# Block products from the ninth and the fifth feature tile on, h shifted by ScalarE, and two side jobs moved into the down projections

## The chip, the cores and the metric

The kernel runs on one core of a Trainium2 chip. Five engines with queues of their own work at once: TensorE (PE in the profile; its weight loads are listed apart as PEld), VectorE (DVE), ScalarE (ACT), GpSimd (POOL) and SyncE (SP), which here issues nearly all transfers. The metric is the device time of one execution in microseconds, taken as the median of several runs.

## The reference

One layer of a streaming encoder with 512 tokens and a model width of 1024, in float32:

```
mod = silu(c) @ w_ada + b_ada                      # nine vectors of 1024: shift, scale, gate, three times
x += 0.5 * g1 * SwiGLU(rms(x) * (1 + s1) + sh1)    # first FFN,  1024 -> 2 x 2816 -> 1024
x += g2 * mixer(rms(x) * (1 + s2) + sh2)           # gated DeltaNet heads and latent attention heads
x += 0.5 * g3 * SwiGLU(rms(x) * (1 + s3) + sh3)    # second FFN, same sizes
SwiGLU(h) = (silu(h @ w_gate) * (h @ w_up)) @ w_out
```

The change touches the two FFNs and the small work that runs beside them, not the mixer itself.

## The kernel before

**Layout.** Everything is kept transposed: 128 features on the partitions, the 512 tokens along the free dimension. So h is eight tiles of 128x512, and the 2816 hidden features are 22 feature tiles, numbered from 0.

**Precision.** Each float32 operand is split into a rounded part and a rest, and each product is three matmuls: high by high, high by low, low by high (`mm3`, L447 to L449). h is held as pairs hh, hl. `modulated` makes them: VectorE scales x into a scratch tile hm (L639), ScalarE adds the shift and rounds to hh (L641), VectorE makes hl (L633). A weight tile is split by ScalarE (a rounding copy, L217) and VectorE (the rest, L218).

**Ordinary feature tiles** (`plain`, and the end of `by_sevens`): gate and up are two accumulators, each of 8 x 3 matmuls of 512 columns. `glu` applies silu on ScalarE (L808) and multiplies on VectorE (L810). There are three accumulators in PSUM for all of this.

**Product tiles** (`by_sevens`, `seven_products`, `sevenths`): gate and up together are seen as a 2 by 2 block matrix, tokens halved as well, and are made from seven block products instead of eight, each of 4 x 3 matmuls of 256 columns (L335). For this VectorE and ScalarE form four sums of weight blocks (s12, s34; L252, L256, L267, L276), and `combined` forms once per FFN four sums of blocks of h, the tiles t7. `combined` first gets h back as hh + hl (L303). `SEVEN` holds the range of feature tiles that are done so: 9 to 18 in the first FFN, 5 to 18 in the second. Tiles 0 to 2 of the first FFN are done by the opening stage (`phase0`), 19 to 21 are ordinary again; during those `parted` splits all finished activations (`glu_parts`, L816, L817).

**Down projections** (`down`): eight output tiles, each of three weight units with 8, 8 and 6 of the 22 feature tiles, three matmuls of 512 columns for each. At the end VectorE adds the gated result to x (L922); the second FFN then transposes and stores the tile (`store`, L992, L994). The last output tile is done in two halves.

**Side work.** Small jobs are written as generators and put into `Side` lists, which the loops step between groups of matmuls; `Rates` steps a list at a given rate. They are:
- `ada_rest`: the remaining columns of `mod`. It streams w_ada (tiles ar), accumulates it on VectorE (aa, L762, L764), sums over partitions with TensorE (L783), copies the row out of PSUM (rw, L786) and transposes it (L790). Group 0 holds the first gate, group 3 the last gate, which `down` of the second FFN needs.
- `mixer_consts`: positions, cosine and sine tables and gains for the mixer; 14 small loads, 58 VectorE instructions, 32 small fills on GpSimd.

Group 0 runs beside the ordinary tiles of the first FFN, groups 1 and 2 in its down projection. `mixer_consts` runs beside tiles 19 to 21 of the first FFN, group 3 beside tiles 19 to 21 of the second and the start of its down projection.

**Order.** A planner orders each engine's instructions, in the main by their place in the program, and takes later ones first where it holds earlier ones to be unready. `in_order`, `behind` and `queued` fix the order of some of them. Tiles come from pools: 56 slots of 128x512 for h, activations and scratch, four buffers each for raw, high and low weights; the pools early (first column group) and seven (weight sums) follow each other in the same memory.

Of the kernel before, what the change touches and what calls it, by code (L numbers as in the profile page):

```python
# [20 lines left out]
NT = 512  # L21
# [8 lines left out]
SEVEN = range(9, 19), range(5, 19)  # L30
# [59 lines left out]
class Block:  # L90
# [201 lines left out]
    def combined(self):  # L292

        nc, v = self.nc, self.nc.vector
        f = lambda x: x.bitcast(F32)
# [3 lines left out]
        for j in range(4):  # L299
            x = []  # L300
            for h in (self.h[j], self.h[j + 4]):
                x.append(self.slot(s="hx"))
                v.tensor_tensor(out=x[-1], in0=f(h[0]), in1=f(h[1]), op=ALU.add)  # L303
# [173 lines left out]
    def phase0(self):  # L477
# [66 lines left out]
        nc.vector.tensor_tensor(out=hl, in0=m, in1=hh.bitcast(F32), op=ALU.subtract)  # L544
        nc.vector.tensor_tensor(out=wl, in0=raw0, in1=wh.bitcast(F32), op=ALU.subtract)
        raw(*tiles[7])
        pu = [self.acc() for _ in range(3)] + [self.aux() for _ in range(3)]
        for kt in range(KT):
# [9 lines left out]
            for j in range(6):  # L558
# [4 lines left out]
                if j == 2 and more:  # L563
                    columns(kt + 1, *cols)
                    self.modulate([kt + 1], slice(0, NT), rb, self.c2, self.c1)
                    if kt == 0:
                        w = weights(kt + 1)
# [35 lines left out]
    def new_h(self):  # L603
        self.h = [(self.slot(F32R, "hh"), self.slot(F32R, "hl")) for _ in range(KT)]

# [16 lines left out]
    def modulate(self, kts, ts, rb, scale, shift):  # L622
        drain(self.modulated(kts, ts, rb, scale, shift))

    def modulated(self, kts, ts, rb, scale, shift):
# [5 lines left out]
        def low(kt, t):  # L631
            hh, hl = self.h[kt]
            nc.vector.scalar_tensor_tensor(out=hl[:, ts], in0=t[:, :w], scalar=shift[:, kt:kt + 1],  # L633
# [3 lines left out]
        for kt in kts:  # L637
            t = self.slot(s="hm")
            nc.vector.scalar_tensor_tensor(out=t[:, :w], in0=self.xT[kt][:, ts], scalar=scale[:, kt:kt + 1], in1=rb[:, :w],  # L639
                                           op0=ALU.mult, op1=ALU.mult)  # L640
            nc.scalar.activation(self.h[kt][0][:, ts], t[:, :w], AF.Identity, bias=shift[:, kt:kt + 1])  # L641
# [40 lines left out]
    def norm_half(self, half, pc, j):  # L682
# [10 lines left out]
        yield from self.modulated(range(KT), ts, rb, self.mod[j + 1], self.mod[j])  # L693
# [83 lines left out]
    def ada_columns(self, g, accs):  # L777
# [8 lines left out]
        nc.vector.tensor_copy(rw[:32 * n, :], pr[:32 * n, :])  # L786
# [48 lines left out]
    def ffn1(self):  # L835
# [1278 lines left out]
```

## Time and profile before

| | us |
|---|---|
| median of three runs | 1058.62 (1057.68 to 1059.16) |
| profiled execution, its own time | 1057.94 |
| span of its profile | 1056.2 |
| first FFN, product tiles 9 to 18 | 133.1 to 234.0 |
| first FFN, tiles 19 to 21 | 234.0 to 267.3 |
| first down projection | from 267.3 |
| second FFN, product tiles 5 to 18 | 748.8 to 889.9 |
| second FFN, tiles 19 to 21 | 889.9 to 925.8 |
| second down projection and stores | from 925.8 |

Times inside the span count from its start. In a group row the columns are line, engine, operation, tiles, count, then busy time and mean duration, then the idle time ahead of it and what ended that. In a timeline row they are start, duration, engine, line, tiles. Matmuls overlap, so the distance of their starts is what they cost, not their listed duration. In a row of windows stand the stretch, its length, then busy time (and count) of TensorE, its weight loads, VectorE, ScalarE and GpSimd, the granted TensorE clock, the busy share of the DMA engines and GB/s.

### The profile page before, as it was taken

The page shows a single profiled execution, that of the slowest core. Times are in us where ns is not written, and L with a number is a line of the kernel's source. Part 1 is how long each engine was busy: PE and PEld are TensorE (multiplying, and loading weights), DVE is VectorE, ACT ScalarE, POOL GpSimd, SP SyncE. Part 2 cuts the span into 40 slices and gives each one's busy share as a digit, 9 for nine tenths or more (in the row PEclk, how much of TensorE's full clock was granted, in tenths as well). Part 3 has the DMA queues.
Part 4 walks back from the last instruction along what each step waited for, and adds up shares of the span by engine and source line. Part 5 has one row for each costly group of instructions (what it writes and reads, how often), then busy time and mean ns, then how long its engine had stood idle before and what let it go on. Part 6 is the DMA issues. An engine that isn't in the chain of part 4 may idle for free.

```text
span 1056.2 us, 16319 instructions
## 1 busy us (share of the span) xinstructions
PE 1035.7 (98%) x6417; PEld 904.3 (86%) x6417; DVE 722.5 (68%) x1280; ACT 471.2 (45%) x857; POOL 25.2 (2%) x74
## 2 busy tenths in 40 slices
PE   6999999999999999999999989999999999999998
PEld 5788799998887798888788769998999999778887
DVE  4479978769888547558787477788688886842221
ACT  3342345555222225469864554354455556422221
POOL 0000000000100000100000001100000000000000
PEclk8999999999999999999999999999999999999999
DMA  9988234343789435211232021113333344723320
GB/s 276 285 260 278 82 100 119 102 121 91 256 287 339 130 96 158 78 40 41 61 80 66 21 80 41 40 42 99 98 103 101 102 119 141 227 76 111 112 62 30
DMA packets 208028, 130.74 MB, mean 124 GB/s; under 512 B 13890, under 2 KB 192079, under 8 KB 207951
## 3 DMA queue, kind: packets, MB, share of 16 engines
q1 hardware_dynamic: 207950, 129.69, 41.3%
q8 instruction: 50, 0.82, 0.3%
q14 instruction: 28, 0.22, 0.1%
HBM read 127.18 MB, written 2.49 MB: 123 GB/s over the span
## 4 chain that ended last, share of the span: by engine, by line
PE 89%; DVE 5%; ACT 2%; DMA 2%; issue 2%; SPq 0%; POOL 0%; DVEq 0%; POOLq 0%; ACTq 0%
PE pa L447 18%; PE pa L448 18%; PE pa L449 18%; PE pa L335 13%; PE pb L335 10%; PE pb L447 1%; PE pb L448 1%; PE pb L449 1%; PE pb L596 1%; PE pb L1847 1%; DVE wl L218 1%; PE pb L1827 1%; DMA xt<-in_x 0%; DVE cv L1391 0%; ACT bd L1477 0%
## 5 line engine op out<-in xcount | busy, mean ns | idle before, releaser
L217 ACT CAST wh<-wr 128x1024 fp32r<-128x1024 f32 (+1 forms) x116 | 116.4, 1008 | 245.8 <-PE pa L448 216.7
L218 DVE TENSOR_TENSOR wl<-wr,wh 128x1024 fp32r<-128x1024 f32 (+1 forms) x116 | 135.3, 1169 | 117.5 <-ACT wh L217 113.3
L447 PE MATMUL pa<-hh,wh 128*128 128x512 f32 (+1 forms) x453 | 174.8, 386 | 1.6 <-ACT sg L808 1.6
L448 PE MATMUL pa<-hl,wh 128*128 128x512 f32 (+1 forms) x453 | 172.8, 381 | 0.0
L449 PE MATMUL pa<-hh,wl 128*128 128x512 f32 (+1 forms) x453 | 172.7, 381 | 0.0
L447 PE MATMUL pa<-ah,wh 128*128 128x512 f32 (+1 forms) x396 | 146.6, 370 | 0.0
L449 PE MATMUL pa<-ah,wl 128*128 128x512 f32 (+1 forms) x396 | 144.9, 366 | 0.0
L448 PE MATMUL pa<-al,wh 128*128 128x512 f32 (+1 forms) x396 | 144.8, 366 | 0.0
L447 PEld LDWEIGHTS pa<-hh,wh 128*128 128x128 f32 x453 | 85.3, 188 | 20.7 <-ACT sg L808 3.0
L449 PEld LDWEIGHTS pa<-hh,wl 128*128 128x128 f32 x453 | 85.3, 188 | 15.8 <-DVE wl L218 0.4
L448 PEld LDWEIGHTS pa<-hl,wh 128*128 128x128 f32 x453 | 85.4, 188 | 14.3 <-DVE hl L633 0.2
L447 PEld LDWEIGHTS pa<-ah,wh 128*128 128x128 f32 x396 | 74.7, 189 | 14.3 <-ACT wh L217 1.7
L449 PEld LDWEIGHTS pa<-ah,wl 128*128 128x128 f32 x396 | 74.7, 189 | 12.3
L448 PEld LDWEIGHTS pa<-al,wh 128*128 128x128 f32 x396 | 74.7, 189 | 11.8
L764 DVE SCALAR_TENSOR_TENSOR aa<-ar,sc,aa 128x512 f32<-128x512 f32 x98 | 73.0, 749 | 9.3 <-DMA ar<-in_w_ada 7.7
L252 DVE TENSOR_TENSOR wl<-sf,wh 128x1024 fp32r<-128x1024 f32 x48 | 58.6, 1222 | 30.0 <-ACT wh L256 30.0
L335 PE MATMUL pa<-hh,wh 128*128 128x256 f32 x192 | 54.5, 284 | 0.0
L335 PE MATMUL pa<-th,wh 128*128 128x256 f32 x192 | 54.3, 283 | 0.0
L335 PE MATMUL pa<-tl,wh 128*128 128x256 f32 x192 | 54.3, 283 | 0.0
L335 PE MATMUL pa<-th,wl 128*128 128x256 f32 x192 | 54.3, 283 | 0.0
L335 PE MATMUL pa<-hl,wh 128*128 128x256 f32 x192 | 54.3, 283 | 0.0
L335 PE MATMUL pa<-hh,wl 128*128 128x256 f32 x192 | 54.3, 283 | 0.0
(434 smaller groups left out, 2214.1 us busy)
## 6 DMA issues: line engine op xcount, KB each, us to landing
wr<-in_ffn_w_in SPq DMA_DIRECT2D x79, 512.0 KB, 3.8
ar<-in_w_ada SPq DMA_DIRECT2D x80, 256.0 KB, 5.9
ar<-in_w_ada SPq DMA_DIRECT2D x32, 512.0 KB, 7.6
wr<-in_ffn_w_out SPq DMA_DIRECT2D x32, 512.0 KB, 3.9
wr<-in_w_in SPq DMA_DIRECT2D x21, 512.0 KB, 3.7
wr<-in_ffn_w_out SPq DMA_DIRECT2D x16, 384.0 KB, 3.6
wr<-in_w_out SPq DMA_DIRECT2D x8, 512.0 KB
wr<-in_ffn_w_in SPq DMA_DIRECT2D x8, 384.0 KB, 7.0
```

Of the source, the lines that this page charges most:

```text
L217: self.nc.scalar.copy(hi, raw)
L218: self.nc.vector.tensor_tensor(out=lo, in0=raw, in1=hi.bitcast(F32), op=ALU.subtract)
L252: sub = lambda out, x, y: nc.vector.tensor_tensor(out=out, in0=x, in1=y, op=ALU.subtract)
L335: nc.tensor.matmul(z, a[:, j, :], b, start=start and j == 0 and i == 0, stop=j == 3 and i == 2, skip_group_check=not start)
L447: mm(out, wh, xh, start=start, stop=False)
L448: mm(out, wh, xl, start=False, stop=False)
L449: mm(out, wl, xh, start=False, stop=stop)
L596: nc.tensor.matmul(pg[32 * q:32 * q + 32, :256], self.sc[:, kc:kc + 1].to_broadcast([P, 32]), a[:, kc], start=(e == 0), stop=(e == 1), til ...
L764: nc.vector.scalar_tensor_tensor(out=acc, in0=a, scalar=sc, in1=acc, op0=ALU.mult, op1=ALU.add)
L1827: nc.tensor.matmul(ps[:, :n], self.qnT[h][:, ts], self.knT[h][:, :n], start=True, stop=False)
L1847: nc.tensor.matmul(po[:, :P], pT[:, b * P:(b + 1) * P], v[b][:, h * P:(h + 1) * P], start=(b == 0), stop=(b == i))
```

## The change

- `SEVEN` begins one tile earlier in both FFNs: tile 8 in the first and tile 4 in the second become product tiles. The ordinary stretches ahead of them shorten by one tile, and the rates of the side work there are set anew; the first column group is flushed one tile earlier.
- `combined` no longer adds hh + hl on VectorE. `modulated` keeps its scratch tile hm (`self.kept`), and ScalarE adds the shift to it in place. For tile 0 of the first FFN the already shifted tile m is kept.
- In `ada_columns`, ScalarE copies the row out of PSUM in place of VectorE.
- `mixer_consts` moves from tiles 19 to 21 into output tiles 3 and later of the first down projection.
- Group 3 of `ada_rest` moves into output tiles 0 and 1 of the second down projection, at three steps a part. These two tiles' results stay in their accumulators until the gate is there; stores run one tile later.
- In the last product tile the next weight unit is split as that tile's third side step, not ahead of it, and the raw weights of the next tile are requested one tile earlier.

```diff
-SEVEN = range(9, 19), range(5, 19)
+SEVEN = range(8, 19), range(4, 19)
...
     def combined(self):
...
-            for h in (self.h[j], self.h[j + 4]):
-                x.append(self.slot(s="hx"))
-                v.tensor_tensor(out=x[-1], in0=f(h[0]), in1=f(h[1]), op=ALU.add)
+            for k in (j, j + 4):
+                t, shift = self.kept[k]
+                if shift is not None:
+                    nc.scalar.activation(t, t, AF.Identity, bias=shift)
+                x.append(t)
...
     def modulated(self, kts, ts, rb, scale, shift, keep=False):
...
-            t = self.slot(s="hm")
+            if not keep:
+                t = self.slot(s="hm")[:, :w]
+            else:
+                if ts.start == 0:
+                    self.kept[kt] = self.slot(s="hm"), shift[:, kt:kt + 1]
+                t = self.kept[kt][0][:, ts]
...
     def ada_columns(self, g, accs):
...
-        nc.vector.tensor_copy(rw[:32 * n, :], pr[:32 * n, :])
+        nc.scalar.copy(rw[:32 * n, :], pr[:32 * n, :])
...
     def ffn1(self):
...
-            self.plain(act, 3, 5, Rates((side,), (0.75,)))
-            self.plain(act, 5, 6, Rates((side, sums), (0.75, 1)))
-        self.plain(act, 6, 8, Rates((side, sums), (1, 1)))
+            self.plain(act, 3, 4, Rates((side,), (0.75,)))
+            self.plain(act, 4, 6, Rates((side, sums), (0.75, 1)))
+        self.plain(act, 6, 7, Rates((side, sums), (1, 1)))
         side.flush()
         self.late_exit()
         self.seven_enter()
-        self.plain(act, 8, 9, sums, True)
+        self.plain(act, 7, 8, sums, True)
         sums.flush()
-        consts = Side()
-        consts.add(self.mixer_consts())
-        self.by_sevens(act, SEVEN[0], consts, 12)
-        consts.flush()
+        self.by_sevens(act, SEVEN[0])
...
     def by_sevens(self, act, fs):
...
+        def first():
+            yield
+            yield
+            self.prefetch(1)
...
             else:
-                self.prefetch(1)
+                side.add(first())
+            if f + 2 == fs.stop:
+                self.preload(2)
...
     def down(self, act, gate, norm=None):
...
+        side, held = Side(), []
+        side.add(self.ada_rest((1, 2) if norm else (3,), True))
+        consts = Side()
         if norm:
-            side = Side()
-            side.add(self.ada_rest((1, 2), True))
+            consts.add(self.mixer_consts())
         for t in range(last):
             if norm and t == 1:
                 self.masks()
-            for i, _ in enumerate(parts(t, full)):
-                side.step((2, 2, 2)[i])
-                if not norm and i == 1 and t > 0:
-                    self.store(t - 1, range(NB))
+            for i, _ in enumerate(parts(t, full, late=not norm and t < 2)):
+                side.step(2 if norm else 3)
+                if t > 2:
+                    consts.step()
+                if not norm and i == 1 and t > 2:
+                    self.store(t - 2, range(NB))
+            if not norm and t == 1:
+                side.flush()
+                for h in held:
+                    finish(*h)
+                self.store(0, range(NB))
...
     def ffn2(self, norms):
...
-        self.plain(act, 2, 4, Rates((side,), (2,)))
-        self.plain(act, 4, 5, side, True)
+        self.plain(act, 2, 3, Rates((side,), (3,)))
+        self.plain(act, 3, 4, side, True)
         side.flush()
-        others = Side()
-        others.add(self.ada_rest((3,), True))
-        self.by_sevens(act, SEVEN[1], others, 8)
-        self.down(act, 8, side=others)
+        self.by_sevens(act, SEVEN[1])
+        self.down(act, 8)
```

More of the change, by code (lines that the diff above doesn't have):

```diff
@@ L692, in norm_half @@
         yield
-        yield from self.modulated(range(KT), ts, rb, self.mod[j + 1], self.mod[j])
+        yield from self.modulated(range(KT), ts, rb, self.mod[j + 1], self.mod[j], j == 6)
     def first_units(self, units, lag, norms):
@@ L913, in by_sevens, with down @@
         side.flush()
-    def down(self, act, gate, norm=None, side=None):
+    def down(self, act, gate, norm=None):
         nc = self.nc
@@ L928, in finish, with parts @@
                 self.square_in(t, ts, accum)
-        def parts(t, ts, units=None, by=8):
+        def parts(t, ts, units=None, by=8, late=False):
             p = self.acc()
@@ L936, in parts @@
                     yield
-            if norm and ts != full:
+            if late:
+                held.append((t, ts, p))
+            elif norm and ts != full:
                 update(t, ts, p)
@@ L956, in down @@
             for i, _ in enumerate(parts(last, ha, units)):
-                if i == 1:
-                    self.store(last - 1, range(NB))
+                if i < 2:
+                    self.store(last - 2 + i, range(NB))
             for i, _ in enumerate(parts(last, hb, units)):
```

22 lines of the change are left out of this document (10 added, 12 removed).

## The prediction

> **What bounds the kernel now.** I read the page first (busy shares and the chain), then TensorE's waits, then the instructions of each stage in order of time, then the stages' busy times.
>
> ```profile
> span 1056.2 us, 16319 instructions
> PE 1035.7 (98%) x6417; PEld 904.3 (86%) x6417; DVE 722.5 (68%) x1280; ACT 471.2 (45%) x857; POOL 25.2 (2%) x74
> PE 89%; DVE 5%; ACT 2%; DMA 2%; issue 2%; SPq 0%; POOL 0%; DVEq 0%; POOLq 0%; ACTq 0%
> ```
>
> TensorE is busy for 98% of the span and holds 89% of the chain that ended last. So the time falls only by TensorE work taken out or by holes closed, and it rises wherever an engine that feeds TensorE comes late. Outside the mixer there are few holes. The largest is in the view of TensorE's waits, and the timelines of TensorE and ScalarE show its place:
>
> ```profile
> PE pa L447 <- ACT sg L808: 1.6, 2, 1.4
> 906.00 0.39 PE L449 MATMUL pa<-hh,wl 128*128 128x512 f32 x1
> 907.80 0.50 PE L447 MATMUL pa<-hh,wh 128*128 128x512 f32 x1 [1.41 <-ACT sg L808]
> 907.15 0.59 ACT L808 ACTIVATE sg<-pa 128x512 f32<-128x512 f32 x1
> 247.46 0.59 ACT L808 ACTIVATE sg<-pa 128x512 f32<-128x512 f32 x1
> 918.91 1.05 PE L783 MATMUL pb<-aa,ones 128*32 128x512 f32 x2
> 920.17 0.50 PE L447 MATMUL pa<-hh,wh 128*128 128x512 f32 x1 [0.22 <-ACT sg L808]
> 936.79 0.98 PE pb L783 x2
> 889.88 0.40 PE L447 MATMUL pa<-hh,wh 128*128 128x512 f32 x1
> 925.75 0.39 PE L447 MATMUL pa<-ah,wh 128*128 128x512 f32 x1
> ```
>
> The hole lies in the second FFN, in the three ordinary feature tiles behind the block products (889.88 to 925.75). Tile 20's second projection needs the accumulator that tile 19's gate still holds, until ScalarE runs its silu (L808) at 907.15. In the first FFN the same silu runs at 247.46, and TensorE does not wait. Starts there are normally 0.23 us apart, so the hole is 907.80 - 906.00 - 0.23 = 1.57 us. At 918.91 a pair of column sums and its hole take 1.26 us to the next start, where such a pair takes 0.98 (the row at 936.79): 0.28 us more.
>
> **Block products in two more tiles.** The price of a tile is read from starts, because matmuls overlap and their mean length is no price.
>
> ```profile
> 250.98 0.39 PE L447 MATMUL pa<-hh,wh 128*128 128x512 f32 x1
> 267.08 0.39 PE L449 MATMUL pa<-hh,wl 128*128 128x512 f32 x1
> 133.10 0.28 PE L335 MATMUL pa<-hh,wh 128*128 128x256 f32 x1
> 141.90 2.88 PE pa L335 x24
> 151.98 2.88 PE pa L335 x24
> 748.79 1.43 PE pa L335 x12
> ```
>
> From 250.98 to 267.08 lie 72 matmuls without a break: 16.10 / 71 = 0.2268 us each. An ordinary tile has 2 x 8 x 3 = 48 of them, 10.88 us. A product tile has 7 x 4 x 3 = 84 matmuls of 256 columns; the same product returns after 151.98 - 141.90 = 10.08 us, 0.120 us each. So each converted tile saves 0.80 us of TensorE, and two save 1.60 us. Weight bytes stay the same. The Trainium skill, TensorE: Matmul & The Clock Gate, Back-to-back issue gap, gives N / 2.4 + 2.5 ns for one warm matmul: as an estimate 215.8 and 109.2 ns here, 10.36 against 9.17 us a tile and 2.4 us saved, which would make the total 0.8 us lower. The trace's 226.8 and 120.0 ns lie 11 ns above both, and the sum goes by the trace.
>
> What this costs is cover. The first product tile comes 10.88 us earlier, with less VectorE time ahead of it.
>
> ```profile
> 62.00:122.40 60.40, 60.40 (x270) 49.02 (x270) 53.44 (x80) 20.67 (x28) 0.00 (x0) 1.00 0.76 235
> 122.40:133.20 10.80, 10.80 (x51) 8.92 (x50) 10.80 (x21) 3.85 (x6) 0.00 (x0) 1.00 0.25 74
> 143.30:153.40 10.10, 10.10 (x87) 10.10 (x86) 8.31 (x13) 5.54 (x10) 0.00 (x0) 1.00 0.35 101
> 716.00:738.00 22.00, 22.00 (x99) 18.22 (x98) 21.66 (x40) 10.19 (x15) 0.00 (x0) 1.00 0.28 80
> 130.44 1.22 DVE L252 TENSOR_TENSOR wl<-sf,wh 128x1024 fp32r<-128x1024 f32 x1
> 744.29 1.23 DVE L252 TENSOR_TENSOR wl<-sf,wh 128x1024 fp32r<-128x1024 f32 x1 [0.95 <-ACT wh L256]
> 122.40 1.28 DVE L303 TENSOR_TENSOR hx<-hh,hl 128x512 f32<-128x512 f32 x2
> L786 DVE COPY rw<-pb x4: 681/684/691, 121.8 to 937.8; 128x512 f32<-128x512 f32 x3, 64x512 f32<-64x512 f32 x1
> L218 DVE TENSOR_TENSOR wl<-wr,wh 128x1024 fp32r<-128x1024 f32 x93 | 113.3, 1222 | 71.1 <-ACT wh L217 69.2 <-PE pb L1528 0.7
> L641 ACT ACTIVATE hh<-hm,sh 128x512 fp32r<-128x512 f32 x7 | 5.1, 725 | 14.0 <-DVE hm L639 14.0
> L994 ACT COPY o<-pb 128x512 f32<-128x512 f32 x7 | 4.1, 583 | 9.7 <-PE pb L992 9.7
> ```
>
> In the rows of windows, VectorE is the fourth column, behind the length, TensorE and its weight loads. In the first FFN, from 62.00 on, where the opening stage ends for it, it works 53.44 of 60.40 us up to 122.40 (6.96 idle) and then without a break until the last weights of the first product tile (130.44 + 1.22 = 131.66): 53.44 + 9.26 = 62.7 us of work. Now there falls away: the two ordinary weight splits of tile 8 (2 x 1.22 = 2.4), the eight sums hh + hl (two take 1.28, overlapping: some 0.60 each, 4.8), and one row copy (0.7). That leaves 54.8 us; with the same idle time the weights are ready at 62 + 54.8 + 7.0 = 123.8. The product tile now starts at 133.10 - 10.88 = 122.2, and the product that needs the last weights is its fourth, 3 x 12 x 0.120 = 4.3 us later, at 126.5. Margin 2.7 us, so I count 0; with no cover at all (the weights at 131.7 as before) it would be 5.2 us. In the second FFN the last weights now come at 744.29 + 1.23 = 745.5, and 7.2 us of work fall away, so 738.3; they are needed 4.3 us behind the new start (748.79 - 10.88 = 737.9), at 742.2: margin 3.9, 0. Behind that, a product tile takes 8.31 us of VectorE in 10.10, and this is unchanged.
>
> ScalarE takes over 7 and 8 shifts of 0.725 us (L641 has their form: a bias, 512 columns) and four row copies of some 0.58 (L994 has their form, out of PSUM). It is busy 3.85 of 10.80 us at the first place and 10.19 of 22.00 at the second, so these are hidden: 0; without that cover 15 x 0.725 = 10.9 us. The kept tiles hold eight slots longer of 56. Beside them stand the 16 h tiles, up to 16 combined ones and 8 activations, and in the second FFN 16 mixed and 12 early weight tiles while h is made: fewer than 56 in both places, 0.
>
> **Constants and last gate's columns moved.** Taking the columns out of 889.88 to 925.75 frees the slots, the accumulations and the DMAs that held back tile 19's silu: 1.57 + 0.28 = 1.85 us gained; bounds 0 (ScalarE's order stays) and 1.85. Their matmuls (two pairs of 0.98 us) remain, later.
>
> ```profile
> 921.00:942.00 21.00, 21.00 (x90) 16.18 (x88) 10.28 (x14) 4.75 (x7) 0.00 (x0) 1.00 0.38 119
> 892.76 0.57 SPq L128 DMA_DIRECT2D ar<-in_w_ada  x1
> 923.95 2.32 DVE L764 SCALAR_TENSOR_TENSOR aa<-ar,sc,aa 128x512 f32<-128x512 f32 x3
> 267.33 0.53 SPq L128 DMA_DIRECT2D ar<-in_w_ada  x1
> 291.62 0.48 DVE L762 TENSOR_SCALAR aa<-ar,sc 128x512 f32<-128x512 f32 x1
> 242.34 0.21 DVE L1048 CAST posf<-posi 4x128 f32<-4x128 int32 x1
> 270.10 0.28 DVE L1076 SCALAR_TENSOR_TENSOR rope<-sin,vb 128x128 f32<-128x128 f32 x1
> L764 DVE SCALAR_TENSOR_TENSOR aa<-ar,sc,aa 128x512 f32<-128x512 f32 x98 | 73.0, 749 | 9.3 <-DMA ar<-in_w_ada 7.7
> ACT wh L217 <- PE pa L448: 216.7, 68, 6.1
> 312.00:357.00 45.00, 45.00 (x205) 36.30 (x204) 35.81 (x50) 10.56 (x12) 0.00 (x0) 1.00 0.81 261
> ```
>
> Where they go: the second down projection now starts at 925.75 - 1.60 - 1.85 - 0.98 = 921.3. Three steps a part put the column sums behind the first part of output tile 1, (22 + 8) x 3 x 0.2268 = 20.4 us later, at 941.7. By then 16 loads of 256 KB must be in and 16 accumulations done. VectorE has room: 10.28 of 21.00 us now, plus ten more accumulations of 0.75 (six lie there already), is 17.8. SP's queue carries the loads between the output weights: 4.2 MB in 20 us is some 200 GB/s on top of the 119 there. The first FFN's down projection did the same eight pairs from 267.33 to 291.62, 24.3 us, with some 4 us of mixer constants and masks in VectorE's way. So 20.3 to 24.3 us against 20.4; TensorE takes other matmuls first if the written order has them, and I count 0, with 3.9 us as upper end. The first two output tiles hold two of three accumulators until then; the third serves tile 2, and tile 3 starts only at 921.3 + 45 = 966. The stores run one tile later, two of them in the last tile's first half; the tail is the same: 0.
>
> The mixer constants (58 VectorE instructions from 242.34 to 270.10, at some 0.25 us 14 us, and eight small loads on SP) move to 312 and later. There VectorE has 9.2 us free up to 357 and more behind it. ScalarE's weight split waits for a buffer that TensorE frees (216.7 us of waiting); with four buffers of 24 matmuls it runs some three units, 3 x 5.44 = 16 us, ahead of its use, which hides a VectorE that lags by 5 us. The constants are needed only in the mixer: 0; up to 2 us if they push back the column sums there. POOL's 32 small fills move too, and nobody waits for them. The last product tile's weight split one step later, and two loads earlier: 0.
>
> **Sum.** 1.60 + 1.85 = 3.45 us. The profiled execution took 1057.94 us (span 1056.2), 0.68 below the median of the runs shown; it becomes 1054.5, and the median 1058.62 becomes 1055.2.
>
> **The rivals.**
> 1. The hole stays: ScalarE puts the next weight split (which waits for TensorE) ahead of the silu for its own reasons. For it: the order on ScalarE is written by a planner, not by this diff. Against it: the first FFN's silu at 247.46 is on time under the same conversions. Time 1058.62 - 1.6 = 1057.0, no measurable change.
> 2. VectorE becomes the bound ahead of the first product tile. For it: it has no idle time from 122.4 to 131.7, and the rest of the first column group is now flushed in one go. Against it: the 2.7 us margin and 7 us of idle time ahead. Stall 1 to 5 us, time 1056.2 to 1060.2, taken as 1058.
> 3. Slower: the column sums of the last gate stand in TensorE's order before their data are there. For it: the loads now run in one burst behind the release of h; before, they took 33.5 us (892.76 to 926.3). At that pace TensorE waits 921.3 + 33.5 - 941.7 = 13 us, time 1068; at the 24.3 us of the first FFN, 3.9 us and 1059. It decides from 20.4 + 5.6 = 26 us on. Against it: the 33.5 us were spread between other work, and the first FFN needed less.
> 4. The weight loads bound short matmuls, so that a product tile is the dearer one. The rows say 10.08 against 10.88, so it has hardly a chance; at 1 us lost it would be 1058.62 - 1.85 + 1.0 = 1057.8. The Trainium skill, in the same section, has a sustained 131 ns at 512 columns and 81 at 128, by which an ordinary tile would be the cheaper one; the trace's 226.8 ns does not agree.
>
> **How the numbers follow.** Forecast 0.55; rival 1 0.17; rival 2 0.14; rival 3 0.12; rival 4 0.02. A measurement of this kernel can tell about 0.2%, 2.1 us: faster means below 1056.5, slower above 1060.7. Faster: the forecast and a small part of rival 2, 0.57. Same: rivals 1 and 4, most of rival 2, part of rival 3, 0.30. Slower: the rest of rival 3 and the end of rival 2, 0.13. The range takes 1.6 us below the forecast for the mixer's order falling out better, and reaches up to 1060.2, the end of rival 2; above it lies most of rival 3. The forecast's own range is 1053.6 to 1056.4.
>
> **What would show it.** TensorE: 26 product tiles of 10.08 us, the first at about 122 and 738; no wait of L447 for L808; no wait in the first product tile for wl (L252) or a combined tile. VectorE: no hx; the first product tile's last weights near 124. Column sums of the last gate near 942 with TensorE going straight on. A wait of TensorE for aa, wl or th of more than 2 us makes the prediction wrong.

## The result and the profile after

| | before | changed |
|---|---|---|
| first series, median | 1058.29 us (6 runs, 1057.1 to 1059.88) | 1054.86 us (6 runs, 1053.79 to 1056.87) |
| ratio, first series | | 0.9969, 95% interval 0.9956 to 0.9982 |
| second series, median | 1057.33 us (32 runs, 1055.0 to 1060.03) | 1056.8 us (12 runs, 1054.78 to 1059.88) |
| ratio, second series | | 0.9997, 95% interval 0.9986 to 1.0008 |
| profiled execution | 1057.94 us | 1056.87 us |

The first series gives the forecast time, 1055.2, almost exactly. The longer second series finds no gain that it can tell from nothing, and the two intervals do not overlap. The profiled pair stands between them, at 1.07 us. What the change does is therefore read from the traces, stretch by stretch, and it is less than the forecast and made of other terms.

The head of the changed kernel's page and its first row of busy times:

```profile
span 1055.2 us, 16491 instructions
PE 1034.8 (98%) x6489; PEld 906.8 (86%) x6489; DVE 719.2 (68%) x1278; ACT 487.1 (46%) x890; POOL 24.9 (2%) x74
```

TensorE is as full as before. In the view of its waits the silu is gone, and a wait for accumulated columns (aa) stands there instead (total, times, longest, in us):

```profile
PE pb L791 <- DVE aa L772: 2.6, 2, 1.6
```

Its timeline shows both places, and the edges of the product tiles (start, duration, then the instruction and what it waited for):

```profile
109.76 1.06 PE L791 MATMUL pb<-aa,ones 128*32 128x512 f32 x6
111.75 1.05 PE L791 MATMUL pb<-aa,ones 128*32 128x512 f32 x2 [0.93 <-DVE aa L772]
112.72 0.50 PE L448 MATMUL pa<-hh,wh 128*128 128x512 f32 x1
124.20 0.28 PE L336 MATMUL pa<-hh,wh 128*128 128x256 f32 x1
235.07 0.40 PE L448 MATMUL pa<-hh,wh 128*128 128x512 f32 x1
738.02 0.28 PE L336 MATMUL pa<-hh,wh 128*128 128x256 f32 x1
889.21 0.40 PE L448 MATMUL pa<-hh,wh 128*128 128x512 f32 x1
942.37 1.04 PE L791 MATMUL pb<-aa,ones 128*32 128x512 f32 x2
943.68 0.40 PE L449 MATMUL pa<-al,wh 128*128 128x512 f32 x1
945.71 1.04 PE L791 MATMUL pb<-aa,ones 128*32 128x512 f32 x2 [1.63 <-DVE aa L772]
946.69 0.50 PE L450 MATMUL pa<-ah,wl 128*128 128x512 f32 x1
```

The product tiles cost what was forecast: (235.07 - 124.20) / 11 = 10.08 us, and (889.21 - 738.02) / 15 = 10.08. But at 109.76 the first gate's column sums take 112.72 - 109.76 = 2.96 us. These are four sums, of which the trace records two matmuls each. In the kernel before all four stood together (x8), and the next matmul started 0.99 us later, at 121.62:

```profile
120.63 1.07 PE L783 MATMUL pb<-aa,ones 128*32 128x512 f32 x8
```

That is 1.98 us lost. And at 943.68 the last gate's sums bring a hole of 945.71 - 943.68 - 0.23 = 1.80 us.

To add it all up, four landmarks are taken that every version has: the last matmul of the opening stage, the `dg` matmuls ahead of the mixer, the `vb,U` matmuls late in the mixer, and the last transposes, with the end of the second FFN's product tiles (889.88 before, 889.21 after) between the last two. First the kernel before, then the changed one:

```profile
65.91 0.39 PE L449 MATMUL pb<-hh,wl 128*128 128x512 f32 x1
400.10 0.67 PE L619 MATMUL pb<-dg,ones 128*128 128x256 f32 x2 [0.78 <-DVE dg L611]
629.26 0.91 PE L1599 MATMUL pb<-vb,U 128*128 128x128 f32 x6 [1.63 <-DVE vb L1179]
1052.47 0.44 PE L992 MATMUL pb<-ident,xT 128*128 128x128 f32 x2 [0.58 <-DVE xT L922]
```

```profile
65.92 0.39 PE L450 MATMUL pb<-hh,wl 128*128 128x512 f32 x1
401.35 0.67 PE L622 MATMUL pb<-dg,ones 128*128 128x256 f32 x2 [0.78 <-DVE dg L614]
629.25 1.02 PE L1618 MATMUL pb<-vb,U 128*128 128x128 f32 x7 [1.65 <-DVE vb L1198]
1051.39 0.44 PE L1013 MATMUL pb<-ident,xT 128*128 128x128 f32 x2 [0.58 <-DVE xT L932]
```

The differences of these starts give the table for every kernel of this study (us; the same landmarks read from each trace). A is the first FFN, B most of the mixer, C the rest of the mixer and the second FFN to the end of its product tiles, D what is left.

| kernel | opening ends | A | B | C | D |
|---|---|---|---|---|---|
| before | 65.91 | 334.19 | 229.16 | 260.62 | 162.59 |
| changed | 65.92 | 335.43 | 227.90 | 259.96 | 162.18 |
| changed, again | 64.91 | 336.09 | 228.29 | 259.92 | 162.09 |
| before, last gate moved alone | 64.91 | 334.22 | 229.42 | 260.61 | 161.23 |
| changed, tiles 8 and 4 ordinary | 66.98 | 334.29 | 229.01 | 260.72 | 161.49 |
| changed, tile 4 ordinary | 64.62 | 334.86 | 228.25 | 260.76 | 161.06 |
| changed, constants back | 67.14 | 337.13 | 228.54 | 259.94 | 161.37 |
| changed, hh + hl on VectorE | 64.81 | 335.74 | 228.41 | 261.81 | 161.59 |
| changed, last gate's loads by GpSimd | 66.07 | 336.39 | 228.41 | 259.95 | 160.27 |
| last gate's sums later | 64.00 | 335.95 | 228.16 | 260.94* | 159.29 |
| both sums later | 66.12 | 334.24 | 228.11 | 260.94* | 159.29 |
| both later, tile 8 ordinary | 64.54 | 334.29 | 228.46 | 259.95 | 159.29 |
| both later, tile 3 too | 64.53 | 334.90 | 227.94 | 259.57 | 159.31 |
| the same, room for the row | 67.49 | 333.52 | 228.38 | 259.59 | 159.29 |

(* with a drop of the clock in it, see the last section.) So between the two profiled executions A got 1.24 us longer, B 1.26 shorter, C 0.66 shorter and D 0.41 shorter: 1.09 us. In the second trace of the changed kernel the sum is only 0.17, since A is another 0.66 longer.

The two stalls are the reason why such sums differ: they come each time, but not at the same size.

- A: five traces have the same work up to the mixer (the changed kernel twice, tile 4 ordinary, loads by GpSimd, last gate's sums later). The first gate's four sums, from the first of them to the next ordinary matmul, take 2.37 to 3.59 us there, and A is 334.86 to 336.39, 0.7 to 2.2 above the kernel before. A less these sums is 332.47 to 332.50 in four of them; the fifth (loads by GpSimd) has 333.13 and one more wait of 0.4 us for a row. In the kernel before it is 334.19 - 0.99 = 333.20.
- D: six traces have the last gate's loads and sums as in the changed kernel (it twice, tiles 8 and 4 ordinary, tile 4 ordinary, constants back, hh + hl on VectorE). TensorE waits for aa there for 0.47 to 1.63 us, and D is 161.06 to 162.18, 0.4 to 1.5 below the kernel before. D less this wait is 160.55 to 160.59 in all six.

### The profile page after: what moved, and what is told of

It reads as the page before. It is cut to its first block, busy times and chain, and to the rows that moved or that the text cites. A ratio compares the mean times of both kernels' runs of the same rounds, so it can differ in the third digit from the quotient of the medians.

```text
span 1055.2 us, 16491 instructions
## 1 busy us (share of the span) xinstructions
PE 1034.8 (98%) x6489; PEld 906.8 (86%) x6489; DVE 719.2 (68%) x1278; ACT 487.1 (46%) x890; POOL 24.9 (2%) x74
## 4 chain that ended last, share of the span: by engine, by line
PE 88%; DVE 6%; issue 2%; DMA 2%; ACT 1%; POOL 0%; SPq 0%; POOLq 0%; ACTq 0%; DVEq 0%
PE pa L448 17%; PE pa L449 16%; PE pa L450 16%; PE pa L336 14%; PE pb L336 11%; DVE aa L772 1%; DMA ar<-in_w_ada 1%; PE pb L1866 1%; PE pb L1846 1%; PE pb L598 1%; PE pb L448 1%; PE pb L449 1%; PE pb L450 1%; PE pb L1466 1%; DVE wl L218 1%
## 5 line engine op out<-in xcount | busy, mean ns | idle before, releaser
L218 DVE TENSOR_TENSOR wl<-wr,wh 128x1024 fp32r<-128x1024 f32 (+1 forms) x112 | 130.4, 1168 | 110.8 <-ACT wh L217 106.2
L448 PE MATMUL pa<-hh,wh 128*128 128x512 f32 (+1 forms) x421 | 162.3, 385 | 0.0
L450 PE MATMUL pa<-hh,wl 128*128 128x512 f32 (+1 forms) x421 | 160.4, 381 | 0.0
L449 PE MATMUL pa<-hl,wh 128*128 128x512 f32 (+1 forms) x421 | 160.4, 381 | 0.0
L448 PEld LDWEIGHTS pa<-hh,wh 128*128 128x128 f32 x421 | 79.4, 189 | 16.5 <-issue 1.7
L450 PEld LDWEIGHTS pa<-hh,wl 128*128 128x128 f32 x421 | 79.3, 188 | 14.5 <-DVE wl L218 0.4
L449 PEld LDWEIGHTS pa<-hl,wh 128*128 128x128 f32 x421 | 79.4, 189 | 13.1 <-DVE hl L636 0.2
L252 DVE TENSOR_TENSOR wl<-sf,wh 128x1024 fp32r<-128x1024 f32 x52 | 63.5, 1221 | 31.7 <-ACT wh L256 31.6
L336 PE MATMUL pa<-hh,wl 128*128 128x256 f32 x208 | 59.0, 284 | 0.0
L336 PE MATMUL pa<-tl,wh 128*128 128x256 f32 x208 | 59.0, 284 | 0.0
```

What stands on the lines that cost most here:

```text
L218: self.nc.vector.tensor_tensor(out=lo, in0=raw, in1=hi.bitcast(F32), op=ALU.subtract)
L252: sub = lambda out, x, y: nc.vector.tensor_tensor(out=out, in0=x, in1=y, op=ALU.subtract)
L336: nc.tensor.matmul(z, a[:, j, :], b, start=start and j == 0 and i == 0, stop=j == 3 and i == 2, skip_group_check=not start)
L448: mm(out, wh, xh, start=start, stop=False)
L449: mm(out, wh, xl, start=False, stop=False)
L450: mm(out, wl, xh, start=False, stop=stop)
```

## The experiments

Each ratio is to the kernel before in the same series. The series ran on different chips, so ratios are compared between them, not medians.

**The changed kernel again.** No edit.

> The changed kernel once more, so that a second trace of it exists. Theory A (the sum of the prediction): 3.45 us faster than the kernel before, and TensorE's stalls before the sums of the first and the last gate's columns, 1.98 us at 109.8 and 1.80 us at 943.7 in the first trace, are chances of that one execution. Theory B: both stalls are part of the order of work and return within 0.3 us, and the profiled pair's 1.07 us is what the trace can account for.

Measured: ratio 0.9997, interval 0.9986 to 1.0008. Both stalls are back:

```profile
108.75 1.06 PE L791 MATMUL pb<-aa,ones 128*32 128x512 f32 x6
111.36 1.04 PE L791 MATMUL pb<-aa,ones 128*32 128x512 f32 x2 [1.56 <-DVE aa L772]
945.60 1.04 PE L791 MATMUL pb<-aa,ones 128*32 128x512 f32 x2 [1.52 <-DVE aa L772]
```

The sums begin 1.0 us sooner here, with the opening stage, but the late pair only 0.4 sooner: the stall is 0.6 us longer. So they belong to the order of work, as theory B has it, though the first changed by more than the 0.3 us that it allowed. Here the opening that ended sooner was partly lost to them.

**Tiles 8 and 4 ordinary again.**

```diff
-SEVEN = range(8, 19), range(4, 19)
+SEVEN = range(9, 19), range(5, 19)
...
-            self.plain(act, 3, 4, Rates((side,), (0.75,)))
-            self.plain(act, 4, 6, Rates((side, sums), (0.75, 1)))
-        self.plain(act, 6, 7, Rates((side, sums), (1, 1)))
+            self.plain(act, 3, 5, Rates((side,), (0.75,)))
+            self.plain(act, 5, 6, Rates((side, sums), (0.75, 1)))
+        self.plain(act, 6, 8, Rates((side, sums), (1, 1)))
...
-        self.plain(act, 7, 8, sums, True)
+        self.plain(act, 8, 9, sums, True)
...
-        self.plain(act, 2, 3, Rates((side,), (3,)))
-        self.plain(act, 3, 4, side, True)
+        self.plain(act, 2, 4, Rates((side,), (2,)))
+        self.plain(act, 4, 5, side, True)
```

> The changed kernel, but tiles 8 and 4 are ordinary again, with the old rates of the side work ahead of them; all other edits stay. Theory A: 1.60 us slower than the changed kernel, 0.80 for each tile. Theory B: the first FFN gets ahead by 1.98 - 0.80 = 1.2 us, since the stall before the first gate's column sums goes, but TensorE waits that much longer for VectorE in the mixer near 559; the second FFN loses 0.7. So 0.7 us slower than the changed kernel, and a hole near 559 of about 1 us as in the kernel before.

Measured: ratio 1.0000, interval 0.9991 to 1.0009. A is 334.29, as before the change and 1.1 to 1.8 below the changed kernel; the stall is gone with the conversion. C is 260.72, 0.76 to 0.80 above it. So the conversion gains its 0.8 us in the second FFN and loses more than that in the first, by the stall. The hole near 560 is back (B 229.01).

**Tile 4 alone ordinary.** The same edit for the second FFN only.

> The changed kernel, with only tile 4 of the second FFN ordinary again (tile 8 of the first stays a product tile). Theory: from the mixer's end to the end of the product tiles 0.7 to 0.8 us more than in the changed kernel, all else the same. Open: the inverse's trip through memory, which stands ahead of the second FFN, took 4.2 to 4.6 us from the first issue to the second in the three traces with tile 4 ordinary, and 2.7 to 2.9 in the nine others. If it goes with where the program and its tiles lie in memory as the second FFN's range sets it, it takes over 4 us here and TensorE waits about 1 us near 560; if those three were chance, it takes 2.7 us.

Measured: ratio 0.9995, interval 0.9985 to 1.0005. C is 260.76, 0.80 to 0.84 above the changed kernel: the product tile's worth. The memory trip took 2.7 us (551.94 to 554.62) and there is no hole near 560, so it does not go with this range alone. All else was not the same: A is 334.86 and D 161.06, 0.6 to 1.2 and 1.0 to 1.1 us below the changed kernel's two traces, because both stalls are smaller in this execution:

```profile
109.85 1.04 PE L791 MATMUL pb<-aa,ones 128*32 128x512 f32 x2 [0.34 <-DVE aa L772]
943.84 1.04 PE L791 MATMUL pb<-aa,ones 128*32 128x512 f32 x2 [0.47 <-DVE aa L772]
```

**The last gate moved, alone.** The kernel before, with the changed `down` (without the constants) and group 3 taken out of the second FFN's tiles.

```diff
-        others = Side()
-        others.add(self.ada_rest((3,), True))
-        self.by_sevens(act, SEVEN[1], others, 8)
-        self.down(act, 8, side=others)
+        self.by_sevens(act, SEVEN[1], Side(), 0)
+        self.down(act, 8)
```

> The kernel before, with only the last gate's columns moved into the second down projection (two output tiles held, stores later). Theory A: 1.85 us faster than the kernel before; the wait for silu near 906 is gone and nothing takes its place. Theory B: the wait near 906 is gone, and one of 1.6 to 1.8 us for the accumulated columns stands near 945 in its place; within 0.3 us of the kernel before.

Measured: ratio 0.9993, interval 0.9981 to 1.0005. The wait near 906 is gone, and this one has come:

```profile
942.32 1.05 PE L783 MATMUL pb<-aa,ones 128*32 128x512 f32 x2
944.68 1.05 PE L783 MATMUL pb<-aa,ones 128*32 128x512 f32 x2 [0.65 <-DVE aa L764]
```

D falls by 1.36 us, not by the forecast's 1.85: the hole here is 0.82 us, where the changed kernel's first trace has 1.8 and others less. So the hole moved and shrank, between the two theories.

**The last gate's sums one unit later.**

```diff
-                side.step(2 if norm else 3)
+                side.step(2 if norm or t or i == 2 else 3)
```

> The changed kernel, with the last gate's column sums one weight unit later in the second down projection (steps of 3, 3, 2, 2, 2, 2 a part in place of 3 each): they come at some 947, where the last accumulation ended at 945.7. Theory A: no difference from the changed kernel. Theory B: the wait of 1.63 us before these sums is gone, and the kernel is 1.6 to 1.8 us faster than the changed one; if the work behind the gate now comes late, a new wait of TensorE for xT or an accumulator stands near 955 to 966 and takes part of it.

Measured: ratio 0.9965, interval 0.9954 to 0.9976, against 0.9997 for the changed kernel in the same series. The two sums (four records, of which the expectations speak) now stand together, and no hole is left:

```profile
947.65 1.05 PE L791 MATMUL pb<-aa,ones 128*32 128x512 f32 x4
```

D is 159.29, 2.9 us less than in the changed kernel's first trace (1.8 to 2.9 less than in the six with its order): 1.80 for the hole, and 0.98 because two sums together take no longer than one, which the expectation had missed. No new wait came.

**The last gate's loads by GpSimd.** The order of the sums stays; only the queue of the sixteen loads is another.

```diff
-                    self.load(a[e], src[e * P:(e + 1) * P])
+                    (self.nc.gpsimd if 3 in groups else self.nc.sync).dma_start(a[e], src[e * P:(e + 1) * P])
```

> The changed kernel, with the sixteen loads of the last gate's columns issued by GpSimd, which has nothing else to do there, in place of SyncE, on whose queue they stand between loads of output weights that wait for a free buffer. Theory B (the queue's order makes the last accumulation late): the loads go out by about 926 in place of 937.6, the wait of 1.63 us before the sums near 943.7 is gone, and the four sums stand together, which saves another 0.98 us: 1.6 to 2.6 us less behind 889 than the changed kernel. Rival (the memory's pace or VectorE makes it late): the loads land no earlier than 941, and the wait stays at 0.6 to 1.6 us.

Measured: ratio 0.9977, interval 0.9967 to 0.9986; D 160.27, 1.9 us below the changed kernel's first trace and 0.8 to 1.9 below the six. First SyncE's queue in the changed kernel, and what it waited for between 915 and 948:

```profile
924.62 3.97 SPq L128 DMA_DIRECT2D ar<-in_w_ada  x8
929.67 5.34 SPq L128 DMA_DIRECT2D wr<-in_ffn_w_out  x2
935.12 2.89 SPq L128 DMA_DIRECT2D ar<-in_w_ada  x6
```

```profile
SPq L128 <- DVE wl L218: 22.4, 6, 6.9
```

then GpSimd's last load, and the sums, in this one:

```profile
926.13 0.76 POOL L756 DMA_DIRECT2D ar<-in_w_ada  x1 [1.79 <-issue]
943.98 2.00 PE L791 MATMUL pb<-aa,ones 128*32 128x512 f32 x4
```

On SyncE six loads stand behind output weights that wait for a buffer which VectorE's split has to free. On GpSimd the last goes out some 11 us sooner (926.1; on SyncE the six go out from 935.12 to 938.0, one after the other). VectorE's last accumulation ends at 944.88, 54.1 us behind the end of the product tiles (890.82); in the changed kernel's first trace it was 945.66, 56.5 behind 889.21. Against the six traces with SyncE's loads the second sum starts 1.2 to 2.4 us sooner behind that end. So the order on the queue made the columns late, though 11 us on the queue bring only this much: what is left is VectorE's, which splits a weight tile until 941.0 and then does the last five accumulations without a break. The hole is gone, but the 0.98 us that the expectation counted on top is not: the second sum waits for the last accumulation and starts at 944.93, behind the first, and the two take 945.91 - 943.98 = 1.93 us to the next matmul.

The Trainium skill, Trainium Kernel Development and Optimization, Key Constraints, says that issuing from several engines at once saves only the sequencer's issue time; read alone, by that nothing should have moved here. These rows do not agree where the first queue's head is waiting for something else.

**Both gates' sums later.** Group 0's accumulated columns lie in slots, and its sums are stepped in tile 7, ahead of which they were flushed.

```diff
+        self.waiting = None
         for g in groups:
...
-                acc = self.slot(s="aa") if late else self.early.tile([P, NT], F32, tag="aa", name=self.name("aa"), bufs=6)
+                acc = self.slot(s="aa")
...
+        if not late:
+            self.waiting = waiting
+            return
         yield
...
         self.seven_enter()
+        sums.add(self.waiting)
         self.plain(act, 7, 8, sums, True)
```

> The kernel with the last gate's sums one unit later, and now the first gate's column sums too stand later in TensorE's order: the accumulated columns of group 0 lie in slots, so that the sums may come in the middle of tile 7, some 5 us later, in place of the end of tile 6. VectorE's work is the same. Theory B (the written order makes the stall): the stall of 2 us near 109 is gone, the first product tile starts near 122 and waits for nothing; 1.98 us faster than with the last gate's sums later alone, so some 2.8 + 2.0 = 4.8 us faster than the changed kernel in the trace. Rival (VectorE is the bound of this stretch): the stall only moves into the first product tile, as a wait for wl or th of 1 to 2 us, and nothing is gained.

Measured: ratio 0.9966, interval 0.9952 to 0.9979, no better than with the last gate's alone (0.9965), though these runs had the lower mean clock (0.9966 against 0.9981). In the trace A is 334.24, 1.7 us shorter than with the last gate's alone. The stall for aa is gone and no product tile waits for weights, so the rival falls: VectorE was late for the sums because they were written early, not for the product tiles. What is left is a wait for ScalarE's copy of the row, which stands behind two weight splits:

```profile
118.10 0.66 PE L802 MATMUL pb<-ident,rw 128*128 128x128 f32 x4 [0.51 <-ACT rw L798]
```

**Tile 8 ordinary, with both sums later.**

> Both sums later, but tile 8 of the first FFN is ordinary again; tile 4 of the second stays a product tile. Theory A: the conversion is worth its 0.80 us here too, less the 0.68 us that TensorE waits for the copied row near 117 in the other kernel: with tile 8 ordinary the first FFN is 0.1 us slower or faster, unless the row is late here as well, then 0.8 slower. If the round trip of the inverse near 553 to 560 goes with the conversion of tile 8, it takes 4.2 to 4.6 us from the first issue to the second here, and TensorE waits about 1 us near 560; if it goes with tile 4, it takes 2.7 us.

Measured: ratio 0.9955, interval 0.9943 to 0.9967. A is 334.29, the same as with tile 8 converted and the row late (334.24): 0.8 us gained, 0.7 lost again. The memory trip took 2.9 us, so it does not go with tile 8 either.

**One more product tile in the second FFN.** Both sums later, `SEVEN` from 8 and 3, `plain(act, 2, 3, side, True)` alone ahead of it.

> Both sums later, and one more product tile: the second FFN's range begins at tile 3. Theory B: VectorE is idle for only 0.64 of the 22 us ahead of the first product tile (716 to 738), and that tile would start 10.88 us earlier with 2 x 1.22 + 0.7 = 3.1 us less work for VectorE; it comes 10.88 - 3.1 - 0.6 = 7.1 us later against TensorE. The first tile's last weights were ready at 736.3 and are needed at 738.0 + 4.3 = 742.3, a margin of 6.0: TensorE waits 1.1 us for 0.80 saved, so 0.3 us slower than with both sums later, between 0.8 faster (no wait) and 2 slower. Rival (the cover isn't VectorE's): no wait, 0.80 us faster.

Measured: ratio 0.9954, interval 0.9941 to 0.9967. TensorE waits for nothing in that stretch; C is 259.57, 0.38 us below 259.95 (C with tile 4 first and no drop of the clock), half of the 0.80. My sum of VectorE's work was wrong: some of the weight sums that it does ahead of the first product tile belong to the second, and they move behind the start. VectorE also stood idle for 3.62 us up to 717.64 in the version with both sums later, waiting for a load, and here its weight sums begin at 710.70. Where the other half of the 0.80 went is not shown.

**Room for the row.** The same, and six steps between the first gate's row and its transposes.

```diff
         nc.scalar.copy(rw[:32 * n, :], pr[:32 * n, :])
         yield
+        if g == 0:
+            for _ in range(6):
+                yield
```

> Both sums later and the product tiles from 8 and 3 on, and now the transposes of the first gate's row come six steps behind the row's copy in place of one. Theory: the waits of 0.5 to 1.2 us for ScalarE's copy of the row near 116 go, 0.7 to 1.3 us less up to the mixer than without it, and the same everywhere else: a ratio to the kernel before of 0.994 to 0.995. If VectorE or ScalarE is late for the first product tile by then, a wait for wl or th there takes it back.

Measured: median 1052.29 us, ratio 0.9942, interval 0.9929 to 0.9956, the lowest ratio of all; its interval excludes 1, but overlaps with that of the version above. A is 333.52: 0.77 us below the version with tile 8 ordinary. No wait for the row is left. With neither stall nor late row the conversion is worth its 0.80 in the first FFN too.

**hh + hl on VectorE again.**

```diff
-            for k in (j, j + 4):
-                t, shift = self.kept[k]
-                if shift is not None:
-                    nc.scalar.activation(t, t, AF.Identity, bias=shift)
-                x.append(t)
+            for h in (self.h[j], self.h[j + 4]):
+                x.append(self.slot(s="hx"))
+                v.tensor_tensor(out=x[-1], in0=h[0].bitcast(F32), in1=h[1].bitcast(F32), op=ALU.add)
...
```

> The changed kernel, but VectorE adds hh + hl again for the eight combined tiles of each FFN (8 x 0.60 = 4.8 us more work for it), and ScalarE's shifts fall away. The prediction's margins (2.7 us in the first FFN, 3.9 us in the second): stalls in the first product tile of 2.1 and 0.9 us, 3.0 us slower than the changed kernel. Theory B: the work stands ahead of the first gate's column sums, so the stall near 110 grows from 2.0 us to between 5 and 7, the first product tile of the first FFN waits for nothing, and that of the second for at most 1 us; 3 to 6 us slower than the changed kernel. Rival (ScalarE's shifts were no help): no difference.

Measured: ratio 1.0025, interval 1.0011 to 1.0040, 2.8 thousandths (3.0 us) above the changed kernel's 0.9997. A is 335.74, no more than in the changed kernel: neither theory's stall in the first FFN came. C is 1.85 to 1.89 longer. TensorE's wait, and ScalarE's rows ahead of it:

```profile
735.17 0.50 PE L446 MATMUL pa<-hh,wh 128*128 128x512 f32 x1 [1.55 <-ACT sg L813]
```

```profile
733.06 0.62 ACT L1190 CAST th<-t 128x512 fp32r<-128x512 f32 x1 [0.85 <-DVE t L296]
733.59 1.04 ACT L256 CAST wh<-sf 128x1024 fp32r<-128x1024 f32 x1
734.53 0.59 ACT L813 ACTIVATE sg<-pa 128x512 f32<-128x512 f32 x1
```

The late VectorE holds up ScalarE, which waits in order for VectorE's t, and behind that stands the silu that frees TensorE's accumulator. The 1.9 us of C are less than the 3.0 between the two ratios; what the rest is stays open.

**Constants back beside tiles 19 to 21.**

```diff
-        self.by_sevens(act, SEVEN[0])
+        consts = Side()
+        consts.add(self.mixer_consts())
+        self.by_sevens(act, SEVEN[0], consts, 12)
+        consts.flush()
...
```

> The changed kernel, with the mixer constants back beside tiles 19 to 21 of the first FFN. The prediction counted the move at 0, with up to 2 us lost by it. Theory A: within 0.3 us of the changed kernel in the trace, no wait of TensorE between 234 and 390 in either. Rival: the constants beside the down projection hold VectorE back there, so that the kernel is up to 2 us faster with them back. If the 14 us of VectorE's work beside tiles 19 to 21 hold up the splitting of the finished activations, TensorE waits near 267 and it is slower.

Measured: ratio 1.0012, interval 1.0000 to 1.0025. A is 337.13, 1.0 to 1.7 us above the changed kernel's two traces. A less the first gate's sums (2.86 us) is 334.27, 1.8 above their 332.5. TensorE has a wait of 0.30 us at 247.77 for a load of the constants, and this one, which neither trace of the changed kernel has; ScalarE's rows follow:

```profile
255.04 0.50 PE L448 MATMUL pa<-hh,wh 128*128 128x512 f32 x1 [1.45 <-ACT sg L816]
```

```profile
253.45 1.04 ACT L217 CAST wh<-wr 128x1024 fp32r<-128x1024 f32 x1 [4.26 <-issue]
254.40 0.59 ACT L816 ACTIVATE sg<-pa 128x512 f32<-128x512 f32 x1
```

The silu stands behind a weight split again, as at 906 in the kernel before. With the old ranges nothing of the kind shows (A is 334.29 with all the other edits and 334.19 in the kernel before), so the move avoids a wait that something else in the change would bring. Which edit that is, the range or ScalarE's and SyncE's new order near the last product tile, was not separated.

## Why the prediction came out as it did

The time of the first series was forecast to 0.4 us, but the second series and the traces do not bear the sum out. Step by step:

- **Product tiles, 1.60 us: right as a price, and half of it arrived.** 10.08 us a tile in both FFNs, 0.7 to 0.8 us of gain in C. In the first FFN A less the sums is 0.7 below the kernel before, and the stall ate it.
- **The cover in the first FFN, margin 2.7 us, counted 0: this step failed, by its place.** Margin was counted at the first product tile's weights (forecast 123.8), and those came early:

```profile
109.37 2.32 DVE L772 SCALAR_TENSOR_TENSOR aa<-ar,sc,aa 128x512 f32<-128x512 f32 x3
119.87 1.23 DVE L252 TENSOR_TENSOR wl<-sf,wh 128x1024 fp32r<-128x1024 f32 x1
735.03 1.23 DVE L252 TENSOR_TENSOR wl<-sf,wh 128x1024 fp32r<-128x1024 f32 x1
```

  The last split ahead of the start ended at 121.1, and at 736.3 in the second FFN (forecast 738.3). From 62 to 121.1 VectorE worked 53.85 us (forecast 54.8) and idled 5.25 (forecast 7.0), so the sum of its work was sound. But the flush of the first column group, one tile earlier, put its sums at 109.8, and VectorE ended the accumulations at 111.7: 2.0 and 2.6 us lost in the two traces, 1.4 to 2.6 over five. Rival 2 names this flush and then prices it at the product tile. The sums were a step that is moved, with a wait of their own.
- **The hole at 906, 1.85 us: right, it went** in every version that moved the columns. D less the new wait is 160.6, 2.0 us below the kernel before.
- **The last gate's columns, 20.3 to 24.3 us against 20.4, counted 0: mis-sized.** The down projection starts at 921.88, and the last accumulations are these:

```profile
921.88 0.39 PE L448 MATMUL pa<-ah,wh 128*128 128x512 f32 x1
```

```profile
941.76 3.90 DVE L772 SCALAR_TENSOR_TENSOR aa<-ar,sc,aa 128x512 f32<-128x512 f32 x5 [1.45 <-DMA ar<-in_w_ada]
```

  They end 945.66 - 921.88 = 23.8 us behind the start, at the first FFN's 24.3 and not at 20.3. Rival 3's mechanism came, at 0.47 to 1.63 us of waiting over six traces. The step had SP's queue as room in GB/s, not as an order with waiting loads in it; the run with GpSimd shows that order at 1.2 to 2.4 us. D gained 0.4 and 0.5 us in the two traces of the changed kernel, and up to 1.5 in the others, in place of 1.85.
- **ScalarE's shifts, 0: right.** TensorE loses no time to them, and with the work on VectorE C is 1.9 us longer. The copy of the row by ScalarE and the earlier weight requests were not run alone; TensorE waits for the row in two later versions, 0.51 and 1.18 us.
- **The constants, 0: right for the move itself.** That leaving them would have cost some 1.8 us beside the other edits was not seen.
- **The mixer: not in the sum.** B is 0.9 to 1.3 us shorter. In it the inverse goes through memory and back: the store (t_d<-bt) and the load (t<-t_d), before and after:

```profile
552.48 1.14 SPq L1501 DMA_DIRECT2D t_d<-bt  x2
556.84 0.37 SPq L1503 DMA_DIRECT2D t<-t_d  x1
```

```profile
553.54 1.14 SPq L1520 DMA_DIRECT2D t_d<-bt  x2
556.23 0.37 SPq L1522 DMA_DIRECT2D t<-t_d  x1
```

  From the first issue to the load it was 4.4 us before and 2.7 after; TensorE's wait of 1.06 us ahead of 560.55 went with that. It was 4.2 to 4.6 in the three kernels with both ranges old and 2.7 to 2.9 in the eleven others, though neither range alone brings it. Why is open; chance is not excluded.

In sum 0.80 + 0.80 + 1.85 was forecast. The two traces show a loss of 1.2 to 1.9 us in A, and gains of 0.9 to 1.3 in B, 0.7 in C and 0.4 to 0.5 in D. The gain in B was in no term of the sum and makes up for much of the loss in A. By the prediction's own mark, a wait for aa of more than 2 us (2.6 in the profile), its working was wrong even where its time was met. So the hit of the first series was luck. What makes that series 3 us faster than the second is not settled; the size of each stall alone differs by over 1 us between executions, and so does the opening.

## What to carry to other kernels

When a step is moved, ask first which consumers in the written order of the bounding engine move with it, and compare for each the time at which it stands there with the time at which its data can be ready; a margin at the next large consumer says nothing about a small one in front of it. A load's time is set by what stands ahead of it on its queue, and a queue whose head waits for a buffer is no free bandwidth. Where an effect is a few us, add up the traces between fixed landmarks, and take the waits out apart: stretches with the same work and no stall agreed within 0.1 us (D 159.29 to 159.31 in five traces, C 259.92 to 259.96 in five), stretches with a stall in them differed by 1.1 and 1.5 us, and the ratio of the same kernel by 3 thousandths between two series.

## What the runs showed of the hardware

**Column sums side by side.** Column sums at different column positions (128x512 in, 32 rows out) cost 0.98 to 0.99 us to the next matmul, whether one stands alone (945.71 to 946.69) or four together (120.63 to 121.62). So each one that is written apart costs as much as all. Side by side needs them ready together: where the second of two waited for its data, the pair took 1.93 us (943.98 to 945.91, with GpSimd's loads). The Trainium skill, TensorEngine Tiling (Array Packing), Key Properties, says that tiles of the array run independently of each other; these rows agree.

**The clock in the opening.** The granted clock between 10 and 30 us differs from run to run of the same kernel. The last three numbers of a row are the clock, the DMA share and GB/s. The changed kernel, and then the same kernel again:

```profile
10.00:20.00 10.00, 7.29 (x42) 5.63 (x41) 6.78 (x20) 3.38 (x8) 1.02 (x1) 0.75 1.14 314
20.00:30.00 10.00, 9.99 (x63) 6.32 (x61) 4.33 (x8) 3.51 (x6) 0.00 (x0) 0.91 1.14 307
```

```profile
10.00:20.00 10.00, 7.47 (x53) 6.14 (x52) 8.27 (x23) 3.87 (x9) 1.02 (x1) 1.00 1.14 314
20.00:30.00 10.00, 9.99 (x68) 6.46 (x67) 5.08 (x10) 3.90 (x7) 0.00 (x0) 1.00 1.13 306
```

The opening ends 1.0 us sooner in the second. In the six traces that show 1.00 in both stretches it ends between 64.0 and 64.9, in the seven with 0.67 to 0.91 in both between 65.9 and 67.5; the one with 0.83 and then 1.00 ends it at 64.8. Of 87 runs of the kernel before, the 25 with a mean clock of 0.999 or more have a median of 1055.96 us, and the 45 with 0.997 or less one of 1058.43: 2.5 us that no edit made. What decides on the clock there is not shown.

**A short drop late in the mixer.** In two of the fourteen traces the clock fell for some us near 630, here in the kernel with the last gate's sums later:

```profile
630.00:632.00 2.00, 2.00 (x12) 2.00 (x11) 1.50 (x2) 0.59 (x1) 0.00 (x0) 0.50 0.00 0
```

It costs 1.0 us: 260.94 against 259.95 in C. It follows a wait of TensorE (1.66 us, up to 628.11), but the other twelve traces have that wait too, 1.63 to 1.66 us, and no drop; so the wait alone does not bring it.
